# One decoder block on one core: U products grouped by width, the norm row copied, low weight parts last, a diagonal on ScalarE, and searches at other queries

## The chip, the cores and the metric

The kernel runs on one core of one Trainium2 chip. The metric is the time of one execution on the device in microseconds (us), the median of several runs. The core has five engines that run side by side, each with its own instruction queue: PE (matrix products; PEld is its weight load), DVE (VectorE), ACT (ScalarE), POOL (GpSimd) and SP, which here only issues DMAs. ACT and POOL issue DMAs too.

## The reference, cut to what matters

One decoder block for 256 tokens of width 1024, everything in float32:

```python
h = rms_norm(x, mix_norm_g)
proj = h @ w_in                       # q_a, k_a, v_a, c_q, c_kv, k_pe, gate_a, gate_b
y_a = moba_attention(rope(q_a), rope(k_a), v_a)
y_b = mla_attention(rms_norm(c_q, q_norm_g) @ w_q_up, rms_norm(c_kv, kv_norm_g) @ w_kv_up, ...)
x = x + (sigmoid(gate_a) * (y_a @ w_branch_a) + sigmoid(gate_b) * (y_b @ w_branch_b)) @ w_out
h2 = rms_norm(x, ffn_norm_g)
q = h2 @ w_query                      # 8 heads, two halves of 128 each
s1, s2 = scores of both halves against 128 sub-keys each
v1, i1 = top_k(s1, 16); v2, i2 = top_k(s2, 16)
best, pos = top_k(v1[:, None] + v2[None, :], 16)          # 16 of 16384 experts for each head
g = softmax(best)
x = x + sum over the chosen experts e of g_e * gelu(expert_u[e] . h2) * expert_v[e]
return rms_norm(x, final_norm_g)
```

The kernel doesn't gather experts: it multiplies h2 with all 16384 rows of `expert_u`, places the gates g with one-hot products (and a table in DRAM), multiplies both, and multiplies the result with all of `expert_v`.

## The kernel before

**Split numbers.** Float32 products are made of rounded parts. A weight unit of 128 x 1024 comes by a DMA on SP (`raw`, line 120), ACT rounds it to `hi` (line 133), and DVE or POOL writes the rest, `lo = raw - hi` (line 137; POOL for the attention gates, branches, queries and the first U units, DVE for the others). Buffers of `raw`, `hi` and `lo` rotate, four of each. Activations are split the same way (`hTh`, `hTl`; `h2h`, `h2l`). Three products make one: th x hi, th x lo, tl x hi (`mm3`, lines 152 to 154).

**Order.** Each engine runs its instructions in the order in which the program writes them; this order is written by hand. Waits between engines are by semaphores.

**The stages in time.** Up to 22.5 us: the inputs, the gain row `gr` of the first norm and the first chunk of `w_in`. The row lies on one partition of `gr`, whose others are cleared by DVE (line 184), and a product with ones spreads it over the partitions (`spread`, line 208). Ahead of it and behind it stand products with a zero tile, whose results nobody reads (`idle`, line 201). `gain_mul` multiplies x by the spread row (line 266), and `x_T` transposes it (line 248). `step` then runs over the weight units of a chunk, with both token tiles t = 0 and 1 in each. To 66.6 us: three more chunks of `w_in`, rotary embedding (`rope`, lines 334 to 341) and the two up-projections, before which `c_q` and `c_kv` are multiplied by their gain rows `gqb` (line 405). To 155 us: sixteen attention heads, with steps of the gate chunks and branches between them. To 193.6: branches, merge and `w_out`. To 200: the norm ahead of the experts; its scale is brought in by a transposing product with a diagonal matrix `dg` instead of the identity (line 250; `dg` is written on line 654 and lies in the place of `gqb`). To 253: sixteen `query(n)` with `scores(n - 1)`, each 24 products of 256 columns and two small ones; `top16` on DVE takes the best 16 of each half's scores. `find()` is a generator of eight search steps on DVE: for four pairs of token tile and head group it adds the candidates (`candidates`, lines 816 to 820), takes the best 16 (`retrieve_top`) and subtracts the greatest (`gate_in`, line 832). Four steps run in the query loop, four between the narrow U blocks behind it. `read()` decodes what was found.

**The U units.** 37 of the 128 units run as narrow blocks (`u_mm`, lines 753 to 755: 24 products of 256 columns); 91 run as wide ones (`u_wide`, lines 768 and 769), for which hi meets h2h and h2l at once in 512 columns and lo meets h2h in 256. These are 336 to 614 us together with 64 one-hot products. Then comes the V stage, 1536 products of 512 columns (line 1096, 637 to 981), and the last norm to 992.4.

Of the kernel before, what the change touches and what calls it, by code (L numbers as in the profile page):

```python
# [20 lines left out]
P = 128  # L21
T = 256
# [20 lines left out]
def block_kernel(ctx, tc, consts, constb, pos, x, g_mix, g_ffn, g_fin, w_in, g_q, w_qup, g_kv, w_kvup,  # L43
# [107 lines left out]
    def mm3(o, sh, sl, mh, ml, start, stop):  # L151
        PE.matmul(o, sh, mh, start=start, stop=False)  # L152
        PE.matmul(o, sh, ml, start=False, stop=False)  # L153
        PE.matmul(o, sl, mh, start=False, stop=stop)  # L154
# [17 lines left out]
    def n4(name):  # L172
        return pb.tile([P, 1024], F32, name=name, tag="n4", bufs=8)
# [6 lines left out]
    ones = pb.tile([P, P], F32, name="ones")  # L180
    nc.gpsimd.memset(ones, 1.0)
    xt = [n4("x0"), n4("x1")]
    gr = n4("gr")
    V.memset(gr, 0.0)
    nc.scalar.dma_start(ident, consts[:, C_ID:C_ID + P])
    nc.scalar.dma_start(gr[0:1, :], g_mix)
    freq = pb.tile([P, 48], F32, name="freq")
    nc.scalar.dma_start(freq, consts[:, C_FREQ:C_FREQ + 48])
    for hf in range(2):
# [8 lines left out]
    def idle(n):  # L198
        o = sct()
        for _ in range(n):  # L200
            PE.matmul(o, zb[:, :P], zb[:, :512], start=True, stop=True)

    idle(4)

    gbp = [acc(), acc()]

    def spread(hf):
        PE.matmul(gbp[hf], ones, gr[:, hf * 512:(hf + 1) * 512], start=True, stop=True)

    spread(0)  # L210
    idle(2)

# [5 lines left out]
    maskb = cb[:, B_MASK:B_MASK + 2 * P]  # L218

    def late_constants():  # L220
        nc.gpsimd.dma_start(gqb[:, :256], g_q.to_broadcast([P, 256]))
        nc.gpsimd.dma_start(gqb[:, 256:], g_kv.to_broadcast([P, 128]))
        nc.gpsimd.dma_start(c16, constb[:, B_I16:B_IOTA])
        nc.gpsimd.dma_start(cb, constb[:, :B_I16])

# [56 lines left out]
    def step(ids, u, nd, w, th, tl, tiles, before=None, ahead=2):  # L282
        nstep[0] += 1
        if nstep[0] > 4 and nstep[0] % 4 == 0:
            clear_gates()
        hi, lo = wget(ids[u], ahead)
        n = 2 if nd > 1 else 1
        for t in range(NT):
            if before:
                before(t)  # L290
            sl = slice(t * P, (t + 1) * P)
            for k in range(n):
                db = n * u + k
                mm3(tiles[t][:, :w], th[:, db, sl], tl[:, db, sl],
                    hi[:, k * w:(k + 1) * w], lo[:, k * w:(k + 1) * w], db == 0, db == nd - 1)

    def chunk(c, between=()):
        tiles = [acc(), acc()]
# [6 lines left out]
    def first_chunk():  # L305

        tiles = [acc(), acc()]
        gain_mul(0, 0)
        gain_mul(1, 0)
        x_T(0, 0)  # L310
        emit_split()
        x_T(1, 0)
        spread(1)
        step(U_C[0], 0, ND, CHUNKS[0], hTh, hTl, tiles, ahead=1)
        gain_mul(0, 1)
        gain_mul(1, 1)
        emit_split()
        step(U_C[0], 1, ND, CHUNKS[0], hTh, hTl, tiles, ahead=0, before=lambda t: t and x_T(0, 1))
        x_T(1, 1)
        step(U_C[0], 2, ND, CHUNKS[0], hTh, hTl, tiles, ahead=1)  # L320
        step(U_C[0], 3, ND, CHUNKS[0], hTh, hTl, tiles)
        row_scales()
        late_constants()
        emit_split()
        return tiles
# [320 lines left out]
    def sq_sum(t, k, last=False):  # L646
        ss = ss2[:, t:t + 1]
        if k == 0:
            V.tensor_scalar(ss, ss, 1.0 / D, EPS, op0=OP.mult, op1=OP.add)
        else:  # L650
            V.scalar_tensor_tensor(ss, ss2[:, 2 * k + t:2 * k + t + 1], 1.0 / D, ss, op0=OP.mult, op1=OP.add)
        if last:
            G.tensor_tensor(ss, ss, small[:, 63:64], op=OP.pow)
            V.tensor_scalar(dg[t], ident, ss, None, op0=OP.mult)

    for hf in range(2):
        out_mm(0, 512 * hf, 512 * hf + 512)
# [105 lines left out]
    def u_wide(j):  # L763
        hi, lo = wget(U_U[j])
        s = sct()
        for b in range(ND):
            bs = slice(b * P, (b + 1) * P)
            PE.matmul(s, hi[:, bs], h2[:, b].rearrange("p z n -> p (z n)"), start=b == 0, stop=False)  # L768
            PE.matmul(s[:, :T], lo[:, bs], h2h[:, b, :], start=False, stop=b == ND - 1)  # L769
        return s  # L770

    def u_sum(s):
# [137 lines left out]
    def find():  # L910

        for b in BO:
            candidates(b)
            retrieve_top(b, 0)
            yield
            retrieve_top(b, 2)
            gate_in(b)
            yield

    def read():  # L920

        for b in BO:
# [13 lines left out]
            yield  # L936
            yield

    for n in range(2 * H):
        query(n)  # L940
        if n:
            scores(n - 1)
        if n == H + 2:
            work = find()
        if n > H + 2 and n < 2 * H - 1:
            next(work)
    done = [0]

# [192 lines left out]
    def last_sum(t, part=None, last=False):  # L1141
        ss = ssf[:, t:t + 1]
        if part is None:
            V.tensor_scalar(ss, ss, 1.0 / D, EPS, op0=OP.mult, op1=OP.add)
        else:
            V.scalar_tensor_tensor(ss, part, 1.0 / D, ss, op0=OP.mult, op1=OP.add)
        if last:
            G.tensor_tensor(ss, ss, small[:, 63:64], op=OP.pow)
# [28 lines left out]
    finish(0, 512, 1024, G, nc.sync)  # L1177
    last_add(1, 512, 768, s1)
    V.tensor_tensor(xr[1][:, 768:], xr[1][:, 768:], yo[1][1][:, 256:], op=OP.add)
    last_sum(1)  # L1180
    last_add(1, 768, 1024, ssl, own)
    last_sum(1, s1)
    last_gain(V, 1, 512, 1024)
    last_sum(1, ssl, True)
# [83 lines left out]
```

## Time and profile before

| what | value |
|---|---|
| median of 3 runs | 994.16 us (992.87 to 994.68) |
| the profiled execution's own time | 994.17 us |
| its span, first to last instruction | 992.4 us |
| mean granted TensorE clock | 0.997 |

How to read it: the span is what the trace shows, in microseconds from its start; some 1.8 us of the time lie around it. A line such as L137 is a line of the kernel. The number of an instruction's idle time stands in square brackets with what ended it (its releaser). The clock is a share of the faster of two levels, 2.4 and 1.2 GHz.

### The profile page before, as it was taken

What the parts mean: (1) busy time and instruction counts of PE and PEld (TensorE: products, weight loads), DVE (VectorE), ACT (ScalarE), POOL (GpSimd) and SP (SyncE); (2) the same over time, 40 slices, a digit from 0 to 9 for tenths busy, and PEclk for the clock granted to TensorE, in tenths of its full rate; (3) what the DMA queues carried; (4) which work ended last, traced back from release to release, by engine and by line L of the source; (5) the groups of instructions that cost most, each with busy time, mean ns of one, the idle gap of its engine ahead of it and who ended that gap; (6) DMA issues with size and microseconds to landing.
All of it is one profiled execution on the core that took longest, in us unless ns stands there. A gap on an engine that the chain in (4) does not pass through costs nothing.

```text
span 992.4 us, 16565 instructions
## 1 busy us (share of the span) xinstructions
PE 974.1 (98%) x5464; PEld 847.8 (85%) x5465; DVE 727.9 (73%) x1652; ACT 578.4 (58%) x1158; POOL 365.5 (37%) x249
## 2 busy tenths in 40 slices
PE   8999999999999999999999999999999999999997
PEld 5778888799999988888888889988888888888886
DVE  5745437758998788888888886677777777777765
ACT  4554453444455578887877785555555555555553
POOL 6645451177737867867877800000000000000001
PEclk9999999999999999999999999999999999999999
DMA  6855457564567888888888966688788878887773
GB/s 213 287 191 149 149 187 253 176 212 151 183 185 203 201 199 193 197 201 201 191 193 201 202 199 197 213 276 239 241 240 242 244 242 244 242 241 241 233 216 130
DMA packets 121367, 208.32 MB, mean 210 GB/s; under 512 B 28129, under 2 KB 73841, under 8 KB 121154
## 3 DMA queue, kind: packets, MB, share of 16 engines
q1 hardware_dynamic: 99648, 197.57, 64.6%
q0 software_dynamic: 16976, 0.96, 6.1%
q10 hardware_dynamic: 4658, 8.75, 2.3%
q8 instruction: 43, 0.70, 0.3%
q14 instruction: 42, 0.34, 0.1%
HBM read 189.20 MB, written 18.02 MB: 209 GB/s over the span
## 4 chain that ended last, share of the span: by engine, by line
PE 90%; DVE 5%; POOL 2%; issue 1%; DMA 1%; ACT 0%; POOLq 0%; ACTq 0%; DVEq 0%
PE acc L1096 35%; PE sc L768 17%; PE sc L769 9%; PE acc L152 4%; PE acc L154 4%; PE acc L153 4%; PE sc L789 3%; PE sc L755 3%; PE sc L753 3%; PE sc L754 3%; PE acc L1012 2%; PE sc L500 1%; DVE gm L808 1%; DVE gm L812 1%; DVE gm L806 1%
## 5 line engine op out<-in xcount | busy, mean ns | idle before, releaser
L137 DVE TENSOR_TENSOR lo<-raw,hi 128x1024 fp32r<-128x1024 f32 (+1 forms) x279 | 340.3, 1222 | 80.3 <-ACT hi L133 78.4
L133 ACT ACTIVATE hi<-raw 128x1024 fp32r<-128x1024 f32 (+2 forms) x323 | 339.3, 1054 | 10.8 <-PE acc L154 9.9
L768 PE MATMUL sc<-h,hi 128*128 128x512 f32 x728 | 260.2, 399 | 0.0
L896 POOL DMA_INDIRECT gd<-gate,addr x128 | 216.8, 1694 | 82.5 <-issue 36.6
L769 PE MATMUL sc<-h,lo 128*128 128x256 f32 x728 | 204.8, 281 | 0.0
L768 PEld LDWEIGHTS sc<-h,hi 128*128 128x128 f32 x728 | 137.3, 189 | 30.6
L1096 PE MATMUL acc<-hi,ah 128*128 128x512 f32 x512 | 157.9, 389 | 0.0
L1096 PE MATMUL acc<-lo,ah 128*128 128x512 f32 x512 | 157.9, 389 | 0.0
L1096 PE MATMUL acc<-hi,al 128*128 128x512 f32 x512 | 157.8, 389 | 0.0
L1139 POOL TENSOR_TENSOR gm<-gm 128x512 f32<-128x512 f32 x1 | 1.3, 1299 | 410.5 <-DVE gm L1135 410.5
L1080 ACT ACTIVATE ah<-gm 128x256 fp32r<-128x256 f32 x128 | 53.4, 418 | 155.6 <-DVE lo L137 91.3
L769 PEld LDWEIGHTS sc<-h,lo 128*128 128x128 f32 x728 | 137.8, 189 | 0.0
L137 POOL TENSOR_TENSOR lo<-raw,hi 128x1024 fp32r<-128x1024 f32 x44 | 104.7, 2388 | 67.6 <-ACT hi L133 61.5
L1096 PEld LDWEIGHTS acc<-lo,ah 128*128 128x128 f32 x512 | 96.1, 188 | 19.9
L1096 PEld LDWEIGHTS acc<-hi,al 128*128 128x128 f32 x512 | 96.1, 188 | 19.8
L1096 PEld LDWEIGHTS acc<-hi,ah 128*128 128x128 f32 x512 | 96.1, 188 | 19.8
L1081 DVE TENSOR_TENSOR al<-gm,ah 128x256 fp32r<-128x256 f32 x128 | 54.4, 425 | 55.8 <-ACT ah L1080 55.6
L755 PE MATMUL sc<-h,lo 128*128 128x256 f32 x296 | 84.7, 286 | 2.1 <-DVE lo L137 2.1
L753 PE MATMUL sc<-h,hi 128*128 128x256 f32 x296 | 84.9, 287 | 0.0
L754 PE MATMUL sc<-h,hi 128*128 128x256 f32 x296 | 84.6, 286 | 0.0
L774 ACT ACTIVATE us<-sc 128x256 f32<-128x256 f32 x91 | 35.0, 385 | 59.3 <-PE sc L769 59.3
L755 PEld LDWEIGHTS sc<-h,lo 128*128 128x128 f32 x296 | 57.6, 195 | 2.3 <-DVE lo L137 2.3
(272 smaller groups left out, 1430.5 us busy)
## 6 DMA issues: line engine op xcount, KB each, us to landing
raw<-in_exp_u_dram SPq DMA_DIRECT2D x128, 512.0 KB
raw<-in_exp_v_dram SPq DMA_DIRECT2D x128, 512.0 KB
raw<-in_w_in_dram SPq DMA_DIRECT2D x28, 512.0 KB
gd<-zero ACTq DMA_DIRECT2D x8, 1024.0 KB
raw<-in_w_pq_dram SPq DMA_DIRECT2D x16, 512.0 KB
rl<-gd SPq DMA_DIRECT2D x128, 64.0 KB
gld<-gs SPq DMA_DIRECT2D x114, 64.0 KB
rl<-gld SPq DMA_DIRECT2D x114, 64.0 KB
```

What stands on the lines that cost most here:

```text
L133: S.activation(hi[:, :w], r[:, :w], AF.Copy)
L137: e.tensor_tensor(lo[:, :w], r[:, :w], hi[:, :w].bitcast(F32), op=OP.subtract)
L152: PE.matmul(o, sh, mh, start=start, stop=False)
L753: PE.matmul(so, hi[:, bs], h2h[:, b, :], start=b == 0, stop=False)
L754: PE.matmul(so, hi[:, bs], h2l[:, b, :], start=False, stop=False)
L755: PE.matmul(so, lo[:, bs], h2h[:, b, :], start=False, stop=b == ND - 1)
L768: PE.matmul(s, hi[:, bs], h2[:, b].rearrange("p z n -> p (z n)"), start=b == 0, stop=False)
L769: PE.matmul(s[:, :T], lo[:, bs], h2h[:, b, :], start=False, stop=b == ND - 1)
L896: i = nc.gpsimd.indirect_dma_start(out=gd[:, :], out_offset=bass.IndirectOffsetOnAxis(ap=addr[g][:, c], axis=0), in_=gate[g][:, c], in_off ...
L1080: S.activation(ah, gm[:, j, :], AF.Copy)
L1081: V.tensor_tensor(al, gm[:, j, :], ah.bitcast(F32), op=OP.subtract)
L1096: PE.matmul(o, st[:, sl], mv[:, c:d], start=j == (0 if own is None else P - LAST) and mv is hi and st is ah, stop=j == P - 1 and st is al)
```

## The change

1. The norm row is loaded into a new tile `g0` by the first DMA of ACT's queue, and two DVE copies bring it to the cleared `gr`. One more product with the zero tile stands ahead of `spread`.
2. The two DMAs of `gqb` go from POOL's queue, behind the first chunk, to SP's, inside it.
3. `step` runs over both token tiles with hi first (two products for each block of 128 rows) and then over both with lo.
4. The diagonal is written by ACT instead of DVE.
5. `u_wide` runs its eight products of 512 columns first and then its eight of 256.
6. The first four steps of `find()` stand behind queries 9, 11, 13 and 15 instead of 11, 12, 13 and 14. Four steps are left behind the loop, as before.
7. In the tail two DVE instructions (`last_sum(1)` and the last `last_add`) change places.

```diff
--- before.py
+++ after.py
@@ -180,10 +180,10 @@
     ones = pb.tile([P, P], F32, name="ones")
     nc.gpsimd.memset(ones, 1.0)
     xt = [n4("x0"), n4("x1")]
-    gr = n4("gr")
+    gr, g0 = n4("gr"), n4("g0")
     V.memset(gr, 0.0)
+    nc.scalar.dma_start(g0[0:1, :], g_mix)
     nc.scalar.dma_start(ident, consts[:, C_ID:C_ID + P])
-    nc.scalar.dma_start(gr[0:1, :], g_mix)
     freq = pb.tile([P, 48], F32, name="freq")
     nc.scalar.dma_start(freq, consts[:, C_FREQ:C_FREQ + 48])
     for hf in range(2):
@@ -200,13 +200,16 @@
         for _ in range(n):
             PE.matmul(o, zb[:, :P], zb[:, :512], start=True, stop=True)
 
-    idle(4)
+    idle(5)
 
     gbp = [acc(), acc()]
 
     def spread(hf):
-        PE.matmul(gbp[hf], ones, gr[:, hf * 512:(hf + 1) * 512], start=True, stop=True)
-
+        cs = slice(hf * 512, (hf + 1) * 512)
+        PE.matmul(gbp[hf], ones, gr[:, cs], start=True, stop=True)
+
+    V.tensor_copy(gr[0:1, :512], g0[0:1, :512])
+    V.tensor_copy(gr[0:1, 512:], g0[0:1, 512:])
     spread(0)
     idle(2)
 
@@ -218,8 +221,6 @@
     maskb = cb[:, B_MASK:B_MASK + 2 * P]
 
     def late_constants():
-        nc.gpsimd.dma_start(gqb[:, :256], g_q.to_broadcast([P, 256]))
-        nc.gpsimd.dma_start(gqb[:, 256:], g_kv.to_broadcast([P, 128]))
         nc.gpsimd.dma_start(c16, constb[:, B_I16:B_IOTA])
         nc.gpsimd.dma_start(cb, constb[:, :B_I16])
 
@@ -284,15 +285,20 @@
         if nstep[0] > 4 and nstep[0] % 4 == 0:
             clear_gates()
         hi, lo = wget(ids[u], ahead)
-        n = 2 if nd > 1 else 1
-        for t in range(NT):
-            if before:
-                before(t)
-            sl = slice(t * P, (t + 1) * P)
-            for k in range(n):
-                db = n * u + k
-                mm3(tiles[t][:, :w], th[:, db, sl], tl[:, db, sl],
-                    hi[:, k * w:(k + 1) * w], lo[:, k * w:(k + 1) * w], db == 0, db == nd - 1)
+
+        for low in range(2):
+            for t in range(NT):
+                if before and not low:
+                    before(t)
+                sl = slice(t * P, (t + 1) * P)
+                o = tiles[t][:, :w]
+                for k in range(2):
+                    db, ws = 2 * u + k, slice(k * w, (k + 1) * w)
+                    if low:
+                        PE.matmul(o, th[:, db, sl], lo[:, ws], start=False, stop=db == nd - 1)
+                    else:
+                        PE.matmul(o, th[:, db, sl], hi[:, ws], start=db == 0, stop=False)
+                        PE.matmul(o, tl[:, db, sl], hi[:, ws], start=False, stop=False)
 
     def chunk(c, between=()):
         tiles = [acc(), acc()]
@@ -318,6 +324,8 @@
         step(U_C[0], 1, ND, CHUNKS[0], hTh, hTl, tiles, ahead=0, before=lambda t: t and x_T(0, 1))
         x_T(1, 1)
         step(U_C[0], 2, ND, CHUNKS[0], hTh, hTl, tiles, ahead=1)
+        nc.sync.dma_start(gqb[:, :256], g_q.to_broadcast([P, 256]))
+        nc.sync.dma_start(gqb[:, 256:], g_kv.to_broadcast([P, 128]))
         step(U_C[0], 3, ND, CHUNKS[0], hTh, hTl, tiles)
         row_scales()
         late_constants()
@@ -651,7 +659,7 @@
             V.scalar_tensor_tensor(ss, ss2[:, 2 * k + t:2 * k + t + 1], 1.0 / D, ss, op0=OP.mult, op1=OP.add)
         if last:
             G.tensor_tensor(ss, ss, small[:, 63:64], op=OP.pow)
-            V.tensor_scalar(dg[t], ident, ss, None, op0=OP.mult)
+            S.activation(dg[t], ident, AF.Copy, scale=ss)
 
     for hf in range(2):
         out_mm(0, 512 * hf, 512 * hf + 512)
@@ -764,9 +772,9 @@
         hi, lo = wget(U_U[j])
         s = sct()
         for b in range(ND):
-            bs = slice(b * P, (b + 1) * P)
-            PE.matmul(s, hi[:, bs], h2[:, b].rearrange("p z n -> p (z n)"), start=b == 0, stop=False)
-            PE.matmul(s[:, :T], lo[:, bs], h2h[:, b, :], start=False, stop=b == ND - 1)
+            PE.matmul(s, hi[:, b * P:(b + 1) * P], h2[:, b].rearrange("p z n -> p (z n)"), start=b == 0, stop=False)
+        for b in range(ND):
+            PE.matmul(s[:, :T], lo[:, b * P:(b + 1) * P], h2h[:, b, :], start=False, stop=b == ND - 1)
         return s
 
     def u_sum(s):
@@ -936,13 +944,12 @@
             yield
             yield
 
+    work = find()
     for n in range(2 * H):
         query(n)
         if n:
             scores(n - 1)
-        if n == H + 2:
-            work = find()
-        if n > H + 2 and n < 2 * H - 1:
+        if n > H and n % 2:
             next(work)
     done = [0]
 
@@ -1177,8 +1184,8 @@
     finish(0, 512, 1024, G, nc.sync)
     last_add(1, 512, 768, s1)
     V.tensor_tensor(xr[1][:, 768:], xr[1][:, 768:], yo[1][1][:, 256:], op=OP.add)
+    last_add(1, 768, 1024, ssl, own)
     last_sum(1)
-    last_add(1, 768, 1024, ssl, own)
     last_sum(1, s1)
     last_gain(V, 1, 512, 1024)
     last_sum(1, ssl, True)
```

PE at the first wide U block: L753 to L755 (L761 to L763 after) are the last narrow block, L1012 (L1019 after) the one-hot products, L768 and L769 (L775 and L777 after) the wide block's products with hi and with lo. Before:

```order
L753 MATMUL sc<-h_73,hi 128x256
L754 MATMUL sc<-h_73,hi 128x256
L755 MATMUL sc<-h_73,lo 128x256
L1012 MATMUL acc<-ow,oi 128x256 x2
L768 MATMUL sc<-h_73,hi 128x512
L769 MATMUL sc<-h_73,lo 128x256
L768 MATMUL sc<-h_73,hi 128x512
L769 MATMUL sc<-h_73,lo 128x256
```

And after:

```order
L761 MATMUL sc<-h_73,hi 128x256
L762 MATMUL sc<-h_73,hi 128x256
L763 MATMUL sc<-h_73,lo 128x256
L1019 MATMUL acc<-ow,oi 128x256 x2
L775 MATMUL sc<-h_73,hi 128x512 x8
L777 MATMUL sc<-h_73,lo 128x256 x8
```

The pair of a wide and a narrow product that stood eight times in a row has become eight wide ones and then eight narrow ones.

SP at the start of the program, whose queue holds only DMA issues: L192 loads x, L120 the weight units. Before:

```order
L192 DMA x_85<-in_x_dram 128x512
L120 DMA raw<-in_w_in_dram 128x832 x2
L120 DMA raw<-in_w_in_dram 128x1024 x8
L120 DMA raw<-in_w_qup_dram 128x768 x2
L120 DMA raw<-in_w_kvup_dram 128x1024
```

And after:

```order
L192 DMA x_85<-in_x_dram 128x512
L120 DMA raw<-in_w_in_dram 128x832 x2
L120 DMA raw<-in_w_in_dram 128x1024 x3
L327 DMA gqb<-in_g_q_dram 128x256
L328 DMA gqb<-in_g_kv_dram 128x128
L120 DMA raw<-in_w_in_dram 128x1024 x5
L120 DMA raw<-in_w_qup_dram 128x768 x2
```

The two loads of gqb stand behind the seventh weight unit, ahead of five others of `w_in`.

ACT ahead of the queries: L133 makes hi, L627 (L635 after) is the square of the norm with its sum, L254 (L255 after) takes the transposed tiles out of PSUM. Before:

```order
L133 ACTIVATE hi<-raw 128x1024 x5
L627 ACTIVATE tg_729,small<-x_1747 128x512 x2
L133 ACTIVATE hi<-raw 128x1024
L627 ACTIVATE tg_730,small<-x_1748 128x512
L627 ACTIVATE tg_730,small<-x_1748 128x256 x2
L254 ACTIVATE h_73<-acc 128x4x128
L254 ACTIVATE h_73<-tr 128x4x128 x2
```

And after:

```order
L133 ACTIVATE hi<-raw 128x1024 x5
L635 ACTIVATE tg_733,small<-x_1751 128x512 x2
L662 ACTIVATE gqb<-ident,small 128x128
L133 ACTIVATE hi<-raw 128x1024
L635 ACTIVATE tg_734,small<-x_1752 128x512
L635 ACTIVATE tg_734,small<-x_1752 128x256 x2
L662 ACTIVATE gqb<-ident,small 128x128
L255 ACTIVATE h_73<-acc 128x4x128
L255 ACTIVATE h_73<-tr 128x4x128 x2
```

The two diagonals (L662, written to the place of gqb) stand on ACT now; the second of them is ahead of the first three copies of transposed tiles.

## Rows read from the trace of the kernel before

**Rows 1.** The page's busy times: engine, us, share of the span, instructions.

```profile
PE 974.1 (98%) x5464; PEld 847.8 (85%) x5465; DVE 727.9 (73%) x1652; ACT 578.4 (58%) x1158; POOL 365.5 (37%) x249
```

**Rows 2.** PE's waits by line: us in total, times, longest us.

```profile
PE acc L208 <- DMA gr<-in_g_mix_dram: 2.6, 1, 2.6
PE sc L755 <- DVE lo L137: 2.1, 1, 2.1
PE acc L153 <- DVE lo L137: 2.0, 2, 1.4
PE tr L250 <- DVE gqb L654: 1.5, 1, 1.5
```

**Rows 3.** Timeline at the start: start us, us, engine, line, operation [idle before <-releaser].

```profile
0.73 0.41 ACTq L185 DMA_DIRECT2D ident<-in_consts_dram  x1
...
1.32 1.89 PE L201 MATMUL sc<-zero 128*128 128x512 bf16 x4 [1.32 <-POOL zero L179]
...
1.95 0.49 ACTq L186 DMA_DIRECT2D gr<-in_g_mix_dram  x1
...
5.85 2.04 PE L208 MATMUL acc<-gr,ones 128*128 128x512 f32 x2 [2.64 <-DMA gr<-in_g_mix_dram]
...
7.93 1.29 DVE L266 TENSOR_TENSOR xg<-x,acc 128x512 f32<-128x512 f32 x2 [6.02 <-PE acc L208]
```

**Rows 4.** Timeline from 15.9 to 32.5 us, around the gain row gqb.

```profile
15.97 0.33 SPq L120 DMA_DIRECT2D raw<-in_w_in_dram  x1
...
26.04 0.68 POOL L221 DMA_DIRECT2D gqb<-in_g_q_dram  x1
...
29.73 0.48 DVE L405 SCALAR_TENSOR_TENSOR cn<-cn,small,gqb 128x256 f32<-128x256 f32 x1 [3.36 <-DMA gqb<-in_g_q_dram]
...
31.16 1.22 DVE L137 TENSOR_TENSOR lo<-raw,hi 128x1024 fp32r<-128x1024 f32 x1
...
32.43 0.50 PE L153 MATMUL acc<-lo,hTh 128*128 128x512 f32 x1 [1.37 <-DVE lo L137]
```

**Rows 5.** PE at 55.6 us; then PE's window: stretch, us, busy (instructions), clock, DMA share, GB/s.

```profile
55.60 0.50 PE L152 MATMUL acc<-hi,hTh 128*128 128x512 f32 x1 [0.38 <-DVE vb L465]
...
80.00:180.00 100.00, 100.00 (x554) 1.00 0.60 189
```

**Rows 6.** Timeline at the second diagonal, and ACT at 450 us.

```profile
195.61 2.34 POOL L137 TENSOR_TENSOR lo<-raw,hi 128x1024 fp32r<-128x1024 f32 x1
195.68 2.36 DVE L654 TENSOR_SCALAR gqb<-ident,small 128x128 f32<-128x128 f32 x1 [0.67 <-POOL small L653]
...
450.13 0.68 ACT L1005 ACTIVATE ow<-oj,gTh 128x128 fp32r<-128x128 bf16 x2
```

**Rows 7.** Timeline of DVE and POOL in the searches, and PE's window behind them.

```profile
236.78 0.50 DVE L804 MAX8 gm<-acc 128x8 f32<-128x128 f32 x2 [0.85 <-PE acc L797]
...
263.93 2.42 POOL L137 TENSOR_TENSOR lo<-raw,hi 128x1024 fp32r<-128x1024 f32 x1 [0.47 <-ACT hi L133]
...
264.92 1.50 DVE L816 TENSOR_TENSOR gm<-gm 128x64 f32<-128x64 f32 x1
...
280.00:300.00 20.00, 20.00 (x159) 0.93 0.75 220
```

**Rows 8.** PE's products: page's group; window of L768 alone; chain; PE's timeline.

```profile
L768 PE MATMUL sc<-h,hi 128*128 128x512 f32 x728 | 260.2, 399 | 0.0
...
594.15:613.94 19.79, 19.79 (x56) 10.43 (x56) 1.00 0.64 199
...
206.87 2.87 PE sc L789 x24
...
637.14 343.89 PE acc L1096 x1517
...
636.98 0.63 PE L1096 MATMUL acc<-hi,ah 128*128 128x512 f32 x2
...
638.82 0.62 PE L1096 MATMUL acc<-lo,ah 128*128 128x512 f32 x2
```

## The prediction

> **What bounds the kernel now.** I read the page's busy times first. PE is busy for 974.1 of a span of 992.4 us [rows 1], so at most 18 us can be won by taking idle time out of PE; anything beyond that has to make its instructions cheaper. So the second view is the list of PE's waits [rows 2], where a handful of single stalls make up most of the idle time: 2.6 us on the norm row at the start, 2.0 on two low parts (the longer 1.4), 1.5 on the diagonal, 2.1 on a low part behind the searches. Third come the timelines at these stalls [rows 3, 4, 6, 7], to see what ended each. Last are the rows that price one matmul in a mixed and in an unmixed series [rows 8]. The profiled execution took 994.17 us, 1.8 more than its span, and the median is 994.16, so what is worked out in the trace's frame needs no shift.
>
> **Norm row.** Before, DVE clears gr from 1.00 to 1.91, and only then is its DMA issued (1.95) behind ident's on ACT's queue. PE's L208 starts at 5.85, 3.9 after the issue, having waited 2.64 us [rows 3]. After, g0's DMA needs no clear and is the first on the queue, where ident's stood at 0.73, and two one-partition DVE copies follow. The head of the program is a chain: L208, gain L266 (7.93), transposes, first step. All of it moves up with L208, as long as x and the first weights, which were issued on SP at the same times, are there. A fifth idle matmul now stands ahead of L208: four took 1.89 from 1.32 on, so the fifth ends at about 3.6. Best case: L208 at 3.5 to 3.8, a gain of 2.0 to 2.4 (2.7, the whole wait, is the ceiling). Worst case: g0 also takes 3.9 from its issue, so it lands at 4.63, and a copy costs up to 0.64 (half of L266's 1.29 for two, which have all 128 partitions): L208 at about 5.2, a gain of 0.65. gr was issued behind x, two weight units and ident, g0 is ahead of nearly all of them, so I take the near side, **-2.1**.
>
> **gqb's DMAs on SP.** POOL issues the first at 26.04 and DVE's L405 waits 3.36 us for it, to 29.73. Behind L405 on DVE stands the low part L137 (31.16), and PE stalls 1.37 for that at 32.43 [rows 4]. After, the issues stand on SP right after the seventh weight unit, which is issued at 15.97 [rows 4], some 10 us earlier. They delay the next weight by two issues, each below 1 us like POOL's 0.68, and that weight has to wait for a buffer anyway. With gqb there, L137 starts 3 us earlier, and PE's stall goes: **-1.4**. Low parts last would remove it too (lo is wanted four matmuls later, 0.9, and DVE's rope waits go), so this is safe twice over. POOL's four issues become two, which frees its next scalar steps.
>
> **Low parts last.** Each step now runs both token tiles over hi first and lo after, with the same products. In the first step the other wait on lo (2.0 - 1.4 = 0.6 [rows 2]) goes, but the second tile's product with tl comes sixth instead of ninth, and DVE writes that part of hTl after lo: a wait of like size stands there. I take **+0.2**, between -0.6 (nothing in its place) and +0.6 (the wait comes twice). The first tile of each chunk is finished later, by four matmuls of 0.2267 = 0.907 (the price is 343.89/1517 [rows 8]). Who waits for that is the evacuation: rope on DVE, then POOL, then the low part of the next weight. After the third chunk this chain is tight: PE already waits 0.38 at 55.60 for a DVE copy that stands behind it [rows 5]. I put **+0.6** there, between 0.2 and one whole lateness of 0.9. Under the attention heads from 80 to 180 us PE is busy for all of 100 us [rows 5], so tiles finished later there have work ahead of them: 0.
>
> **Diagonal on ScalarE.** L654 took 2.36 us on DVE for 128x128 elements. It began 0.07 after a POOL split of 2.34 us and ended with it (195.61 + 2.34 = 197.95; 195.68 + 2.36 = 198.04); PE waited 1.50 at 198.18 [rows 2, 6]. On ACT the nearest row is two 128x128 activations in 0.68, 0.34 each [rows 6]. It waits for the same scalar (195.68), so PE can have it at about 196.1, while PE's wait begins only at 198.18 - 1.50 = 196.68, behind its idle matmuls: the stall goes, **-1.5**. If ACT were slowed like DVE, 0.
>
> **Searches spread out.** Four of the eight steps of find() stand in the query loop before and after. They move from queries 11 to 14 to 9, 11, 13 and 15, and start in DVE's idle time there (0.85 us per query at 236.78 [rows 7]). What could be won is large: the searches are the chain that makes the ninth U block's low part late (PE's 2.15 us on L755 [rows 2]), and the granted clock then falls: 0.93 from 280 to 300 us [rows 7]. A mean of 0.93 over 20 us is 2.8 us at the lower of the two levels (0.07 x 20 / 0.5), which costs half of them, 1.4. With the stall 2.1 + 1.4 = 3.5. But DVE's L816, 64 elements wide, took 1.50 from 264.92 and ended (266.42) with a POOL split that ran 263.93 to 266.35 [rows 7]: an add with two SBUF operands doesn't get through while POOL works, and POOL splits a weight in most of the time here. I carried the new order forward by hand: the steps that start 1.7 us earlier meet the POOL splits of the earlier weights and lose it again by the third of them, and from 266.35 on everything stands as before. **0**, with -3.5 as the other end.
>
> **U blocks.** 91 blocks issue eight 512-column products and eight 256-column ones. Before they alternate: 56 first-kind products take 19.79 us with their partners [rows 8], 0.3534 a pair, 2.827 a block, without idle time (0.0 on L768). After they are grouped. Unmixed prices: 24 of 256 columns in 2.87 (0.1196 each), 1517 of 512 in 343.89 (0.2267); eight 512s right behind a run of 256s took 638.82 - 636.98 = 1.84 [rows 8]. A grouped block is 1.84 + 8 x 0.1196 = 2.797, 0.030 less: 91 x 0.030 = **-2.7**. With the steady 0.2267 for all eight it would be 2.770 and -5.1; the other end is 0. I take the value with the transition in it, since each block has one. The Trainium skill ("TensorE: Matmul & The Clock Gate", section "Wait — 56ns, not 53.3ns?") gives a matmul a fixed addition of some 2.5 ns over its columns, whatever stands beside it. By that rule order is worth nothing and the sum would be 990.0; the mixed pair's 0.3534 against 0.2267 + 0.1196 = 0.3463 speaks against it, since no PE wait stands between them.
>
> **Tail.** One small DVE sum is exchanged with its neighbour, both on the same engine: 0.
>
> Sum: -2.1 - 1.4 + 0.2 + 0.6 - 1.5 + 0 - 2.7 = -6.9, so 994.2 - 6.9 = **987.3**.
>
> **Rivals.** *R1, the searches do get ahead:* DVE needs only to slip past one POOL split, then keeps its 1.7 us, the low part comes in time and the clock holds. 987.3 - 3.5 = 983.8. For it: the margins are fractions of a us, and the start moves DVE and POOL against each other. Against it: three splits in a row must be missed. The Trainium skill ("SBUF — State Buffer", section "SBUF: two separate sides") says that whichever of the DVE and GpSimd operations starts first holds the shared port pair for its whole instruction; L816's 1.50 agrees with the losing side of that, and no row here shows DVE winning.
> *R2, order of U products worth nothing:* 987.3 + 2.7 = 990.0. For it: the difference is 30 ns in 2.8 us. Against: rows 8.
> *R3, g0 lands no sooner than gr did:* the start gives 0.65, 987.3 + 1.45 = 988.8. For it: all first transfers share the same DMA engines.
> *R4, slower:* the 0.907 of the first tile reaches PE at each of 12 tile pairs (eight chunks, four branch pairs): 12 x 0.907 = 10.9, in place of 0.6: 997.6. It outweighs the gains of 7.5 from more than 8 of the 12 on. Against: PE is never idle from 80 to 180, where most of them are evacuated.
> *R5, the stalls reappear one step later* (PE's queue is fed by the same DVE low parts, with waits on other rows): 992 to 994.
>
> **Numbers.** Forecast 0.48, with its own range of 985.5 to 988.8; R1 0.18, R2 0.12, R3 0.10, R4 0.05, R5 0.07. The range 983.0 to 991.0 takes in the forecast, R1, R2 and R3, 0.88, and the far ends of the U price (984.9) and the start. What a measurement here can tell is 0.2%, 2 us: faster means below 992.2. Faster 0.88; same 0.07 (R5); slower 0.05 (R4).
>
> **What would show it.** Norm row: PE's first f32 product at 3.5 to 3.8 without a DMA wait, and the first step's start up by 2 us. gqb: no wait on L405's new line, no PE stall near 30. Diagonal: ACT's piece below 0.5 and no PE wait on it. Searches: PE's wait of about 2.1 us on a low part near 275 and a clock of about 0.93 after it mean forecast, neither means R1. U: a block's 16 products in 2.80. First-tile lateness: new PE waits at chunk ends, a few tenths in all. The forecast is wrong if the clock dips at another place, if SP's two extra issues make a weight late, or if the U block's price doesn't fall.

## The result, and the profile after

The changed kernel took 989.18 us (median of 5 runs, 988.06 to 989.6) against 994.47 us (5 runs, 992.87 to 995.04): ratio 0.995, 95% interval 0.9939 to 0.996, some 5 us less. 987.3 was forecast. The profiled execution took 989.41, its span is 987.6 (992.4 before).

The PE's start times in the two timelines show where each part came in; the last column is the change within the stage that ends there:

| PE's first product of | before | after | difference | in the stage |
|---|---|---|---|---|
| the norm row | 5.85 | 3.43 | -2.42 | -2.42 |
| the first chunk | 11.26 | 9.01 | -2.25 | +0.17 |
| the second chunk | 22.52 | 20.52 | -2.00 | +0.25 |
| the third chunk | 35.64 | 33.38 | -2.26 | -0.26 |
| the fourth chunk | 55.60 | 54.34 | -1.26 | +1.00 |
| w_out | 170.84 | 170.01 | -0.83 | +0.43 |
| the first query | 200.00 | 197.42 | -2.58 | -1.75 |
| the ninth U unit | 276.66 | 274.08 | -2.58 | 0.00 |
| the first wide U block | 341.59 | 339.32 | -2.27 | +0.31 |
| the V stage | 636.98 | 631.67 | -5.31 | -3.04 |

The up-projections stand between the third and the fourth chunk. The span is 4.7 shorter before rounding: 0.6 is lost behind PE's last product, from whose end to the span's end it was 6.92 us and is 7.49.

In five of the kernels built later (u_mixed, step_old, find_old, gqb_pool, merged) the stretch from about 290 to 312 us took 11 to 13 us longer, as in some runs of the kernel before beside them, and the readings of their stages leave it out.

The list of PE's waits of the changed kernel (us in total, times, longest us):

```profile
PE sc L763 <- DVE lo L137: 2.5, 1, 2.5
...
PE acc L300 <- ACT hi L133: 1.2, 2, 1.0
PE acc L152 <- DVE rs L344: 1.1, 2, 0.6
...
PE acc L301 <- DVE hTl L256: 0.7, 2, 0.4
PE acc L300 <- DVE vb L473: 0.4, 1, 0.4
PE tr L249 <- DVE xg L267: 0.3, 1, 0.3
PE tr L249 <- DVE cn L413: 0.3, 1, 0.3
```

Of the waits in [rows 2] the norm row's, the diagonal's and L153's are gone, the searches' is still there (2.5 for 2.1), and five small ones have come, on ACT's hi, rope and DVE's products.

The start, as a timeline (answers to [rows 3]):

```profile
0.73 0.53 ACTq L185 DMA_DIRECT2D g<-in_g_mix_dram  x1
...
1.32 2.32 PE L201 MATMUL sc<-zero 128*128 128x512 bf16 x5 [1.32 <-POOL zero L179]
...
2.22 0.42 DVE L211 COPY gr<-g 1x512 f32<-1x512 f32 x1 [0.31 <-DMA g<-in_g_mix_dram]
...
3.43 1.68 PE L209 MATMUL acc<-gr,ones 128*128 128x512 f32 x2
...
5.15 1.29 DVE L267 TENSOR_TENSOR xg<-x,acc 128x512 f32<-128x512 f32 x2 [2.17 <-PE acc L209]
...
8.43 0.80 POOL L369 TENSOR_SCALAR ang<-freq,posf 128x48 f32<-128x48 f32 x2 [0.74 <-DMA freq<-in_consts_dram]
```

g0 is there at 2.22, 1.5 after its issue (gr took 3.9); the idle products, not the row, hold L209. The last line matters later: POOL's rope angles start at 8.43, hardly sooner than the 8.62 of before.

The second chunk, as a timeline (answers to [rows 4]):

```profile
24.04 0.27 POOL L384 TENSOR_SCALAR arg<-arg 128x96 f32<-128x96 f32 x1
...
24.39 0.19 POOL L240 TENSOR_SCALAR small<-small 128x1 f32<-128x1 f32 x1
...
28.34 0.48 DVE L413 SCALAR_TENSOR_TENSOR cn<-cn,small,gqb 128x256 f32<-128x256 f32 x1 [1.84 <-POOL small L241]
...
29.05 0.50 PE L300 MATMUL acc<-hi,hTh 128*128 128x512 f32 x1 [0.18 <-ACT hi L133]
...
30.02 1.22 DVE L137 TENSOR_TENSOR lo<-raw,hi 128x1024 fp32r<-128x1024 f32 x1
```

DVE no longer waits for gqb, but for POOL's row scales, which stand behind the angles in POOL's queue. L413 starts 1.39 earlier than before (29.73), although PE ahead of it is 2.0 earlier: on PE's clock it is later.

The diagonal, as a timeline (answers to [rows 6]):

```profile
194.60 1.24 PE L201 MATMUL sc<-zero 128*128 128x512 bf16 x5
194.84 0.40 ACT L662 ACTIVATE gqb<-ident,small 128x128 f32<-128x128 f32 x1 [0.86 <-POOL small L661]
195.68 1.05 PE L251 MATMUL tr<-gqb,hg 128*128 128x128 f32 x8
```

0.40 on ACT in place of 2.36 on DVE, and PE goes from its idle products straight on.

Two of the searches' adds, with POOL's splits, as a timeline (answers to [rows 7]):

```profile
231.91 2.39 POOL L137 TENSOR_TENSOR lo<-raw,hi 128x1024 fp32r<-128x1024 f32 x1 [0.93 <-ACT hi L133]
...
233.28 1.10 DVE L824 TENSOR_TENSOR gm<-gm 128x64 f32<-128x64 f32 x1
...
248.51 2.39 POOL L137 TENSOR_TENSOR lo<-raw,hi 128x1024 fp32r<-128x1024 f32 x1 [0.93 <-ACT hi L133]
249.11 1.87 DVE L824 TENSOR_TENSOR gm<-gm 128x64 f32<-128x64 f32 x1
```

The first ends at 234.38, POOL's split at 234.30; the second at 250.98 and 250.90. The earlier places meet earlier splits.

The U blocks: the chain's pieces, then PE's window over all wide blocks (its columns as in [rows 5]; answers to [rows 8]):

```profile
339.49 1.84 PE sc L775 x8
341.32 0.95 PE sc L777 x8
```

```profile
339.32:631.67 292.35, 292.35 (x1776) 1.00 0.82 199
```

A block is 1.84 + 0.95, as the prediction put it together from other stages.

### The profile page after: what moved, and what is told of

Same layout as the page of the kernel before. It is cut to its first block, busy times and chain, and to the rows that moved or that the text cites. A ratio compares the mean times of both kernels' runs of the same rounds, so it can differ in the third digit from the quotient of the medians.

```text
span 987.6 us, 16568 instructions
## 1 busy us (share of the span) xinstructions
PE 971.2 (98%) x5466; PEld 847.2 (86%) x5466; DVE 725.4 (73%) x1652; ACT 578.8 (59%) x1160; POOL 367.7 (37%) x247
## 4 chain that ended last, share of the span: by engine, by line
PE 89%; DVE 5%; POOL 3%; DMA 1%; issue 1%; ACT 0%; ACTq 0%; POOLq 0%; DVEq 0%
PE acc L1103 35%; PE sc L775 17%; PE sc L777 9%; PE acc L300 3%; PE acc L298 3%; PE acc L301 3%; PE sc L763 3%; PE sc L797 3%; PE sc L761 3%; PE sc L762 3%; PE acc L1019 2%; PE sc L508 1%; DVE gm L816 1%; DVE gm L820 1%; DVE gm L814 1%; DMA freq<-in_consts_dram 1%
## 5 line engine op out<-in xcount | busy, mean ns | idle before, releaser
L133 ACT ACTIVATE hi<-raw 128x1024 fp32r<-128x1024 f32 (+2 forms) x323 | 338.9, 1053 | 11.0 <-PE acc L301 5.5
L775 PE MATMUL sc<-h,hi 128*128 128x512 f32 x728 | 182.3, 392 | 0.0
L775 PEld LDWEIGHTS sc<-h,hi 128*128 128x128 f32 x728 | 130.9, 189 | 23.4
L777 PEld LDWEIGHTS sc<-h,lo 128*128 128x128 f32 x728 | 99.3, 190 | 7.1
L777 PE MATMUL sc<-h,lo 128*128 128x256 f32 x728 | 101.5, 282 | 0.0
L763 PE MATMUL sc<-h,lo 128*128 128x256 f32 x296 | 84.6, 286 | 2.5 <-DVE lo L137 2.5
L761 PE MATMUL sc<-h,hi 128*128 128x256 f32 x296 | 84.7, 286 | 0.0
L763 PEld LDWEIGHTS sc<-h,lo 128*128 128x128 f32 x296 | 57.5, 194 | 2.7 <-DVE lo L137 2.7
```

Source lines behind the costliest of these rows:

```text
L133: S.activation(hi[:, :w], r[:, :w], AF.Copy)
L761: PE.matmul(so, hi[:, bs], h2h[:, b, :], start=b == 0, stop=False)
L763: PE.matmul(so, lo[:, bs], h2h[:, b, :], start=False, stop=b == ND - 1)
L775: PE.matmul(s, hi[:, b * P:(b + 1) * P], h2[:, b].rearrange("p z n -> p (z n)"), start=b == 0, stop=False)
L777: PE.matmul(s[:, :T], lo[:, b * P:(b + 1) * P], h2h[:, b, :], start=False, stop=b == ND - 1)
```

## The experiments

Stages are compared by PE's start times in each run's own trace. All of these kernels but best1 and best2 ran once.

**Order in the U blocks (u_mixed).**

```diff
         for b in range(ND):
-            PE.matmul(s, hi[:, b * P:(b + 1) * P], h2[:, b].rearrange("p z n -> p (z n)"), start=b == 0, stop=False)
-        for b in range(ND):
-            PE.matmul(s[:, :T], lo[:, b * P:(b + 1) * P], h2h[:, b, :], start=False, stop=b == ND - 1)
+            bs = slice(b * P, (b + 1) * P)
+            PE.matmul(s, hi[:, bs], h2[:, b].rearrange("p z n -> p (z n)"), start=b == 0, stop=False)
+            PE.matmul(s[:, :T], lo[:, bs], h2h[:, b, :], start=False, stop=b == ND - 1)
```

> The changed kernel with the old order in the wide U blocks alone (512 and 256 columns in turn). From the first wide block to the first V product the kernel before took 295.39 us and the changed one 292.35, 3.04 less. If the order of the widths is what made it, this kernel takes 295.4 there and the same as the changed kernel elsewhere, span about 990.6. If a fixed price of each product rules and the 3 us come from something else (the lighter hold on the hi buffers, for instance), it stays at about 292.4 and the span at 987.6.

PE's window over its wide blocks, behind that of the kernel before:

```profile
341.59:636.98 295.39, 295.39 (x1777) 1.00 0.81 197
...
350.96:646.34 295.38, 295.38 (x1776) 1.00 0.78 197
```

295.38 against 295.39 before and 292.35 after, busy throughout: the order of the widths alone makes the 3.0 us.

**Low parts last (step_old)**: the loop over `low` is taken out of `step`.

```diff
-        for low in range(2):
-            for t in range(NT):
+        for t in range(NT):
...
+                mm3(tiles[t][:, :w], th[:, db, sl], tl[:, db, sl],
+                    hi[:, k * w:(k + 1) * w], lo[:, k * w:(k + 1) * w], db == 0, db == nd - 1)
```

> The changed kernel with the old order in the weight steps alone (hi, lo, hi for each block of rows); gqb stays on SP. Theory: finishing the first tile later is what lost 0.96 us between 45 and 54 us and 0.43 between 68 and 170 us, so the first query starts 1.0 to 1.4 us earlier than in the changed kernel (197.42), at about 196.2. Rival: low parts last saved a stall on the eighth low part that comes back here (up to 1.1 us between 20 and 34 us, where PE now waits 0.34, 0.30 and 0.42), and the losses have another cause: the first query at 197.4 to 198.5.

The first query started at 196.97, between theory and rival. The old order is quicker by 0.23 in the first chunk. From the third to the fourth chunk it takes 20.48 us against 20.96: the up-projections take 8.22 (9.14 in the changed kernel, 8.18 before), but the third chunk itself 0.43 more, as two weight loads (PEld) there wait 0.36 and 0.39 us for DVE's low parts. So the theory holds for 0.92 in the up-projections, where PE waits for rope's DVE products, which read the third chunk's tiles.

The 0.43 under the heads comes back whole (0.44), but not for the theory's reason. In the changed kernel it is lost in one step, where the new order begins the second tile two products sooner; PE waits there for the place of its sum, which DVE is still copying out:

```profile
89.03 0.19 PEld L300 LDWEIGHTS acc<-hi,hTh 128*128 128x128 f32 x1 [0.57 <-DVE kbT L489]
```

Between second and third chunk the stall is there, with gqb on SP:

```profile
PE acc L153 <- DVE lo L137: 2.4, 2, 1.8
```

So moving gqb without the new order doesn't remove it.

**gqb on POOL (gqb_pool)**: the two issues back in `late_constants`.

```diff
     def late_constants():
+        nc.gpsimd.dma_start(gqb[:, :256], g_q.to_broadcast([P, 256]))
+        nc.gpsimd.dma_start(gqb[:, 256:], g_kv.to_broadcast([P, 128]))
...
-        nc.sync.dma_start(gqb[:, :256], g_q.to_broadcast([P, 256]))
-        nc.sync.dma_start(gqb[:, 256:], g_kv.to_broadcast([P, 128]))
```

> The changed kernel with gqb's two DMAs back on POOL behind the first chunk. The prediction said that low parts last alone removes the stall of 1.37 us, so that the third chunk (33.38 us in the changed kernel) starts at the same time within 0.3. Rival: what holds PE between 28 and 33 us is the chain of POOL's small row scales and DVE's products with gqb, which the two issues (0.68 and 0.56 us) and the landing push back; then the third chunk starts 1 to 2.5 us later, at 34.4 to 35.9, and the span grows by as much.

The third chunk started 14.01 us after the second, at 34.37, and DVE's wait is back in full, with 0.9 of it passed on to PE's low parts:

```profile
30.07 0.48 DVE L413 SCALAR_TENSOR_TENSOR cn<-cn,small,gqb 128x256 f32<-128x256 f32 x1 [3.36 <-DMA gqb<-in_g_q_dram]
```

```profile
PE acc L300 <- DVE lo L137: 0.9, 1, 0.9
```

As a time of the stage this is not conclusive: five kernels with the same code there (the changed one, u_mixed, find_old, pool_u9, diag_dve) took 12.86, 12.17, 13.27, 12.26 and 13.96 us for it. But in all five the third chunk starts 9.06 to 9.08 us behind the end of POOL's last angle instruction (24.31, 23.31, 24.63, 23.73 and 24.62), so POOL's series sets it. Measured from there, gqb_pool takes 9.86: the DMAs on POOL cost 0.8 us. step_old takes 10.20, so the old order costs 1.1, and the kernel before, with both, 12.21.

**The norm row alone (start_only)**: the kernel before with the first part of the change.

```diff
-    nc.scalar.dma_start(gr[0:1, :], g_mix)
+    nc.scalar.dma_start(g0[0:1, :], g_mix)
...
-    idle(4)
+    idle(5)
...
+    V.tensor_copy(gr[0:1, :512], g0[0:1, :512])
+    V.tensor_copy(gr[0:1, 512:], g0[0:1, 512:])
```

> The kernel before with the norm row's copy and the fifth idle product alone. The prediction's term stands for itself: the second chunk starts 2.2 us earlier than before (22.52), at 20.3, and all of it is kept, span 990.2. Rival: the rope angles on POOL don't move, so that gqb's issue behind them stays where it was and the stall on the eighth low part grows by what was won; the third chunk (35.64 before) would start at 35 or later and the span be 991.5 to 992.4.

The second chunk started at 19.79, 2.7 earlier than before; the third at 35.58, 0.06 earlier. PE's waits, and its window from 28 to 36 us:

```profile
PE acc L153 <- DVE lo L137: 3.1, 2, 2.5
```

```profile
28.00:36.00 8.00, 5.46 (x21) 0.79 0.71 239
```

The stall grew by 1.2 to 2.5, and the granted clock fell behind it to a mean of 0.79 over these 8 us; that is some 3.4 us at the lower of the two levels, at most 1.7 lost. POOL's angles ended at 23.27 (23.43 before). Span 992.3: the start alone is worth nothing. The rival's times hold; of its mechanism, the longer stall is less than half of what was lost, and the clock is the rest.

**Rope angles begun earlier (angles)**: freq's and the positions' loads ahead of ident's on ACT's queue.

```diff
-    nc.scalar.dma_start(ident, consts[:, C_ID:C_ID + P])
...
     nc.scalar.dma_start(freq, consts[:, C_FREQ:C_FREQ + 48])
+    nc.scalar.dma_start(posi, pos)
+    nc.scalar.dma_start(ident, consts[:, C_ID:C_ID + P])
...
-    nc.gpsimd.dma_start(posi, pos)
```

> The changed kernel with the loads of freq and of the positions ahead of ident on ACT's queue (the positions came over POOL's queue). Theory: what kept PE waiting between 28 and 33 us is POOL's series of rope angles, which began at 8.43 with freq's landing although PE's start had moved up by 2.3; begun 1.5 to 3 us earlier it frees the row scales, and the three waits of 0.34, 0.30 and 0.42 us go: from the second to the third chunk (12.86 us) about 11.6 to 11.9. Rival: ACT's squares or DVE's low parts set it and nothing changes (12.2 to 13.3, as in the kernels of the batch before, whose starts were alike), or ident lands later and the first step moves down by up to 1 us.

```profile
PE tr L249 <- DMA ident<-in_consts_dram: 3.6, 1, 3.6
```

ident came last and cost 3.6; the first chunk began at 12.13. From the second to the third chunk it took 11.49, as the theory has it, but POOL's angles began no earlier than in the changed kernel (8.54 against 8.43), and PE had itself been moved back against POOL by 3.1. So the edit doesn't do what it was meant to, and the run doesn't tell apart what set the stage.

**Fewer instructions for the angles (merged).**

```diff
-kk = pb.tile([P, NT, 48], F32, name="kk")
+kk = pb.tile([P, 2, NT, 48], F32, name="kk")
...
         for w in range(2):
-            G.tensor_scalar(kk, ang, 1.0 / (2 * math.pi), 0.25 if w == 0 else 0.0, op0=OP.mult, op1=OP.add)
-            G.tensor_scalar(kk, kk, MAGIC, None, op0=OP.add)
+            G.tensor_scalar(kk[:, w], ang, 1.0 / (2 * math.pi), 0.25 if w == 0 else 0.0, op0=OP.mult, op1=OP.add)
+        G.tensor_scalar(kk, kk, MAGIC, None, op0=OP.add)
...
```

> The changed kernel with POOL's series of rope angles made for sine and cosine at once: twelve instructions of 192 columns in place of twenty of 96 that took 0.3 to 1.3 us each. Theory: POOL's series holds the row scales back and with them ACT, DVE's products with gqb and PE; it now ends 4 us or more earlier, behind the squares of x, so the three waits of PE between 28 and 33 us (0.34, 0.30, 0.42 in the changed kernel) go. From the second to the third chunk 11.5 to 11.8 us in place of 12.2 to 13.3. Rival: the squares on ACT, which are ready at 20.6 to 21.8, or ACT's order set it; then 12 or more.

11.48 us from the second to the third chunk, about what its 48 products and six transposes need (48 x 0.2267 + 0.66 = 11.54), and no PE wait in it. POOL's timeline:

```profile
20.47 1.01 POOL L382 TENSOR_SCALAR arg<-arg 128x192 f32<-128x192 f32 x1
21.56 0.19 POOL L240 TENSOR_SCALAR small<-small 128x1 f32<-128x1 f32 x1
```

The angles began at 9.47, later than in the changed kernel, and were done 2.8 earlier (21.48 against 24.31). best1 and best2 below, with the same angles, take 11.50 for this stage. POOL's series was the bound. With low parts last kept, the up-projections take 8.40 here, where the changed kernel took 9.14: POOL's lateness has a share in that loss too.

**The searches where they were (find_old).**

```diff
-    work = find()
     for n in range(2 * H):
...
-        if n > H and n % 2:
+        if n == H + 2:
+            work = find()
+        if n > H + 2 and n < 2 * H - 1:
             next(work)
```

> The changed kernel with the search steps behind queries 11 to 14 as before. Theory: the adds wait for POOL's splits wherever the steps stand, so PE's wait on the ninth unit's low part stays near 2 to 2.5 us and the clock falls once behind it for 3.4 us; span 987.3 to 987.8. Rival: the new places win DVE time that is then lost elsewhere; the wait would be 4 us or more and the span about 989.3.

```profile
PE sc L763 <- DVE lo L137: 2.4, 1, 2.4
```

From the ninth to the tenth unit 6.83 us; 7.05 in the changed kernel, 6.78 before; to the eleventh 9.71, 9.96 and 9.65. diag_dve, with the new places, takes 6.78 and 9.65 as well. The new places are worth nothing, and at most cost 0.3.

**Ninth and tenth low part on POOL (pool_u9).**

```diff
-    lo_eng.update({U_U[j]: True for j in range(NP)})
+    lo_eng.update({U_U[j]: True for j in range(NP + 2)})
```

> The changed kernel with the low parts of the ninth and tenth U unit written by POOL instead of DVE. Theory: PE's wait of 2.5 us at the ninth unit and the 3.4 us at half clock behind it come only from DVE being late with that low part; POOL has it by about 272.4 (its last split ends at 269.5), before PE wants it (274.6). Both go: from the ninth to the eleventh unit 5.8 us instead of 9.96, 4.1 less, span about 983.5. Rival: DVE's lateness only moves on to the eleventh unit, or POOL's longer hold on the adds makes it later; then a wait of 2 us or more stands there and little is won.

```profile
PE sc L763 <- DVE lo L137: 1.1, 2, 0.9
```

PE's window from 272 to 288 us, in the changed kernel and here:

```profile
272.00:288.00 16.00, 13.54 (x100) 0.89 0.51 147
...
272.00:288.00 16.00, 14.94 (x123) 1.00 0.57 171
```

The ninth unit took 2.88 instead of 7.05 and the clock stayed at 1.00. 1.6 of the 4.2 won was given back by the eleventh and twelfth units (3.33 and 4.00), where DVE is late again: the theory's cause, and in part the rival's "moves on". Span 984.3, 3.3 less; 0.7 of it was there ahead of the ninth unit.

**The diagonal back on DVE (diag_dve).**

```diff
-            S.activation(dg[t], ident, AF.Copy, scale=ss)
+            V.tensor_scalar(dg[t], ident, ss, None, op0=OP.mult)
```

> The changed kernel with the diagonal back on DVE. Theory: the wait of 1.5 us and the late transposes behind it come back whole, since POOL's split runs at the same time: from the diagonal's first use to the first query 6.35 us instead of 4.60, the span 1.75 more. Rival: the shifts ahead of it have moved DVE's instruction out of POOL's split, and at most 0.3 comes back.

6.34 us from the diagonal's first use to the first query, against 4.60, and the wait is back:

```profile
PE tr L251 <- DVE gqb L662: 1.5, 1, 1.5
```

**All of it together (best1, best2).** best1 has merged's angles, POOL's low parts up to the twelfth U unit, and low parts last in the second chunk alone.

```diff
-    lo_eng.update({U_U[j]: True for j in range(NP)})
+    lo_eng.update({U_U[j]: True for j in range(NP + 4)})
...
+        if ids in (U_C[1],):
+            order = [(t, low) for low in range(2) for t in range(NT)]
+        else:
+            order = [(t, 2) for t in range(NT)]
```

> The changed kernel with the merged rope angles, with four low parts more on POOL (the ninth to the twelfth U unit), and with low parts last in the second chunk alone. Theory: the waits between 28 and 33 us go (about 1.0), the old order gives back 0.23 in the first chunk, about 0.5 from 45 to 54 and 0.44 under the heads, and the ninth unit's wait, the half clock and the twelfth unit's wait that was left with two low parts on POOL go (4.9): 7.0 less than the changed kernel, about 982.2. Rival: the gains don't add up, as those of the norm row and of gqb did not; then 984 to 986.

1106.55 us, ratio 1.1045 (1.0985 to 1.1105). POOL's queue says why:

```
L137 TENSOR_TENSOR lo<-raw,hi 128x1024 x27
L907 DMA gd<-gate_1892,addr_1894 2097152x1 x64
L137 TENSOR_TENSOR lo<-raw,hi 128x1024
L907 DMA gd<-gate_1893,addr_1895 2097152x1 x64
```

```profile
PE sc L766 <- POOL lo L137: 120.8, 1, 120.8
```

The twelfth low part stands behind 64 indirect DMAs, and PE waited for them. Neither theory had that. best2 leaves the twelfth on DVE and has low parts last in the second to fourth chunks:

```diff
-    lo_eng.update({U_U[j]: True for j in range(NP + 4)})
+    lo_eng.update({U_U[j]: True for j in range(NP + 3)})
...
-        if ids in (U_C[1],):
+        if ids in (U_C[1], U_C[2], U_C[3]):
```

> The changed kernel with the merged rope angles, three low parts more on POOL (the ninth to the eleventh U unit, all of them ahead of the gates' indirect DMAs in POOL's queue, where the twelfth stood behind 64 of them), and low parts last in the second to fourth chunks alone. Theory: about 1.4 us before the third chunk, 0.2 in the first, 0.4 under the heads, and 4.2 at the ninth and tenth U units are won against the changed kernel, and the twelfth unit's wait is 0 to 0.9: about 983 where the kernel before takes 994.3, ratio 0.988 to 0.990. Rival: with the earlier units won, DVE's low parts for the twelfth to fourteenth unit are late by as much and 985 to 987 is left.

984.87 us against 993.54 on the same chip: ratio 0.9908, 0.9892 to 0.9925, between the theory's 983 and the rival's 985. By their ratios to the kernel before it is ahead of the changed kernel (0.995, 0.9939 to 0.996). From the ninth to the thirteenth unit it takes 14.04 us, where pool_u9, with one low part less on POOL, took 13.09, so the eleventh low part on POOL doesn't seem to pay; it was not tried by itself. PE's wait for the twelfth unit's low part is what the rival said:

```profile
PE sc L766 <- DVE lo L137: 1.9, 1, 1.9
```

## Why the prediction was right, and where it was not

The median lies in the range and in the direction forecast; the sum was 1.9 too good. In the trace the misses come to 2.9 us, and 0.7 came back where terms did better than forecast, so that the sum is so near is in part luck.

- *Norm row, -2.1:* right, -2.25 at the first chunk; g0 came long before the idle products ended, so R3 is out. But it was priced as if the whole program moved up with it. Alone it gives nothing (start_only): POOL's angles end where they did (23.27 for 23.43), PE's stall behind them grows by 1.2, and half clock for 3.4 us takes most of the rest.
- *gqb's DMAs, -1.4:* this term failed; the stage gained 0.26 [rows 4]. The DMA was the wait that ended last, with POOL's row scales just behind it, and moving PE up by 2 us made these the bound. The step that I left out is asking when POOL would have the scales. From the end of POOL's angles to the third chunk it is 9.07 us now and was 12.21, 3.1 less by gqb and low parts last together; but the angles end 0.88 later (24.31 for 23.43) while PE is 2.0 earlier, and that takes 2.9 of it. merged shows what was under it: 11.48 in place of 12.86. "Safe twice over" is wrong too: with gqb on SP and the old order a stall of 1.8 stands, with the new order and gqb on POOL one of 0.9.
- *Low parts last, +0.2 and +0.6:* +0.25 in the first chunk, right; a wait of 0.44 on hTl stands in the place of that on lo, and a second, of 0.27, was not forecast. The first tile's lateness came to +1.0 by 54 us, nearly all in the up-projections (9.14 for 8.18). It takes two to make it: the old order brings them to 8.22, and POOL's shorter angles, with the new order kept, to 8.40. "0 under the heads" is wrong by 0.43: the prediction asked who waits for the first tile that is finished later, but not for what the second tile waits that begins sooner. R4's mechanism so costs at most 1.0 in all, not 10.9.
- *Diagonal, -1.5:* -1.75, and 1.74 came back in diag_dve. Right.
- *Searches, 0:* right for the reason given. The adds end with POOL's splits at their new places as well, so R1 is out; the row's 1.87 us for 64 columns agrees with the lock that the Trainium skill ("SBUF — State Buffer", section "SBUF: two separate sides") describes. That DVE's lateness with the ninth low part costs the wait and the clock is shown by pool_u9.
- *U blocks, -2.7:* -3.04, with u_mixed giving all of it back. A grouped block takes 2.827 - 3.04/91 = 2.794 where 2.797 was worked out; 91 times the difference is the 0.3 missing. (The far end, with the steady price, comes to 5.2, not 5.1.) R2, the fixed price of the Trainium skill ("TensorE: Matmul & The Clock Gate", section "Wait — 56ns, not 53.3ns?"), doesn't carry over to this mix of widths: 16 products of the same widths cost 3.0/91 = 0.033 us less in the other order.
- *Tail, 0:* 0.6 lost, 0.2 ahead of the end of DVE's last instruction and 0.4 between it and the span's end, in which the last stores land. Neither is chance. From PE's last product to DVE's last instruction, end to end, it takes 3.21 us in the two kernels without the exchange (the one before and start_only) and 3.41 or 3.42 in all eleven with it. Behind DVE it is 3.70 or 3.71 in the three kernels with gqb's DMAs on POOL (these two and gqb_pool) and 4.05 to 4.07 in the ten with them on SP. So the exchange costs 0.2, and the 0.4 goes with two more DMAs on SP; by what way stays open.

## What to carry to other kernels

Two stalls that end at different engines don't add up: before a start is moved up, ask for each engine what starts its own series (here a small load for POOL) and whether that moves too. A stall behind a late load is worth only the distance to the next wait on the same instruction. Where a stage's time scatters from kernel to kernel, measure it from the instruction that sets its end: 12.17 to 13.96 us became 9.06 to 9.08. And before work is given to an idle engine, read its queue: one split behind 64 indirect DMAs cost 120 us.

## What the runs showed of the hardware that was not expected

- Products of 512 columns behind ones of 256 are slower for a while: eight of them take 1.84 against 8 x 0.2267 = 1.81, and in strict alternation a pair costs 0.3534 against 0.3463 [rows 8].
- A load of 1 KB in many small pieces (the positions) and freq, put ahead of ident on one queue, made ident 3.6 us late for PE.
- POOL's small instructions are held up beside DVE's splits as DVE's adds are beside POOL's. In the changed kernel an angle instruction of 96 columns (L380) takes 0.45 us at 21.16, with no DVE work beside it, and 1.30 here, ending 0.3 behind DVE's split:

```profile
21.78 1.39 DVE L137 TENSOR_TENSOR lo<-raw,hi 128x1024 fp32r<-128x1024 f32 x1 [1.49 <-ACT hi L133]
...
22.18 1.30 POOL L380 TENSOR_SCALAR kc<-kk 128x96 f32<-128x96 f32 x1
```

- A stall of 2.5 us brought a stretch of half clock (start_only 0.79 from 28 to 36 us); of 1.4 us in the same place it didn't (kernel before, 1.00 in that window), nor did the 1.8 of step_old there or the 1.9 of best2 at the twelfth unit.
- Behind the start of POOL's indirect DMAs PE is busy for all of 24 us at full clock in the changed kernel, with 209 GB/s moved; in step_old, with the same code there, it is busy for 17.86 of them at a clock of 0.72, with 107 GB/s:

```profile
290.00:314.00 24.00, 24.00 (x202) 1.00 0.75 209
...
290.00:314.00 24.00, 17.86 (x101) 0.72 0.40 107
```

What brings it on stays open.
